# Summing the squares of the token norms on four column tiles and transposing the sums into columns, in a two-layer hybrid decoder trunk

## The chip, the cores and the metric

One core of one Trainium2 chip runs the whole program. The metric is the device time of one launch in microseconds (us), the median of several runs. A profiled execution is read beside them: it has its own time, a span from its first to its last instruction, and a trace of every instruction on the engines TensorE (PE; its weight loads are PEld), VectorE (DVE), ScalarE (ACT), GpSimd (POOL) and SyncE (SP, which issues the transfers).

## The reference, cut to what matters

The trunk has two layers over 512 tokens of width 1024. Each layer has a mixer (gated linear attention, mLSTM and Mamba-2 SSD, merged by gates) and a gated MLP with a causal convolution; both start from an RMSNorm of the residual stream.

```python
def rmsnorm(x, g):
    xf = x.astype(jnp.float32)
    y = xf * lax.rsqrt(jnp.mean(xf * xf, axis=-1, keepdims=True) + EPS)
    return (y * g).astype(x.dtype)

def reference(...):
    h = x
    for l in range(DEPTH):
        h = h + mixer_layer(rmsnorm(h, norm_mix[l]), w_in[l], ...)
        h = h + conv_ffn(rmsnorm(h, norm_ffn[l]), w_up[l], ...)
    return rmsnorm(h, norm_final)
```

The change touches the mean of squares and the inverse root of four of these five norms: the one ahead of the mixer and the one ahead of the MLP, in each of two layers. The final norm has its own code.

## The kernel before, in words

Activations lie with the channel on the partitions and the token along the free axis: 8 tiles of 128 x 512. Products are made in three passes of a split type: each float32 operand is cut into a high part and a remainder (`uh`/`ul` for activations, `wh`/`wl` for weights), and `wh x uh`, `wh x ul` and `wl x uh` are added in PSUM (`prods`). One unit of output, 128 channels by 512 tokens from 8 input tiles, is therefore 24 matmuls of 128 x 512.

The weights come from DRAM as raw tiles (`raw`, three buffers). Each is split on chip by `prep_`: ACT writes the high part (`wh`, line 354, seen in the trace as L230) and DVE the remainder (`wl`, line 355, seen as L233). A chunk is two units' weights; `wh` and `wl` have two buffers each (`W_BUFS = 2`), so the split of chunk c can start only when PE has read the last of chunk c - 2.

The norm's scale is not applied ahead of the products. The products use `h` times the gain, and each unit's result is multiplied by the inverse root (`rstd`, 128 x 512) when it leaves PSUM (`first`: the tiles `sm`, `cx`, `G` and others). While the tiles of `h` come, `square_tile` adds up their squares into one 128 x 512 tile `sq`. Then:

- `norm_end` (line 472) sums `sq` over its 128 partitions with `colsum` (line 790): for each of four blocks of 128 tokens one matmul with the block of `sq` as the weights and a column of ones as the moving operand, so that the sums land as four columns of 128 tokens (`m<-cst,sq`, 128 x 1). DVE scales them (`nx`, line 477) and makes the inverse root in ten short instructions (`rsqrt`, line 486: `rcol`, `nt`).
- `norm_rows_of_cols` (line 482) spreads the four columns `rcol` over all partitions with four transposes on PE (`m<-cst,rcol`, line 245), and ACT copies the result to `rstd`.

Both are called in `units` at a boundary, the first two units of a stage, as `mid`: `norm_end` in the middle of the pair, `norm_rows_of_cols` behind it. The instructions are placed on their engines by a scheduler, from the order of the program, the priorities that the code sets (`high_priority`) and the buffers, so a change in one place can move rows in others.

PSUM has two pools of four buffers, `pacc` (tiles `acc`) and `pm` (tiles `m`). Norm sums and transposes are always taken from `pm`. A unit's accumulator comes from `acc()`, and where `self.wide` is set (the first pair of a layer and the whole MLP) the pool depends on a running count of names:

```python
    def acc(self):
        self.n += 1
        if self.wide and self.n % 2:
            return self.mps()
        return self.pacc.tile([P, T], F32, tag="acc", name=f"acc_{self.n}")
```

`mps()`, `small()` and `t()` each add one to the same count. The column-tiled sum that the change uses is already in the kernel: `sums` (line 714) adds up squares for the heads' norms (`m<-sqo,cst`, 128 rows by 32 columns of weights, 128 moving columns). A float32 matmul shows as two records in the trace, a transpose as one.

Of the kernel before, what the change touches and what calls it, by code (L numbers as in the profile page):

```python
# [13 lines left out]
ALU = mybir.AluOpType  # L14
# [3 lines left out]
P = 128  # L18
L = 2
D = 1024  # L20
T = 512
KT = D // P
NB = T // P
EPS = 1e-6
# [109 lines left out]
class Kern:  # L134
# [337 lines left out]
    def norm_end(self):  # L472

        ps = self.mps()
        self.colsum(ps, 0, self.sq)
        x, rc, s = (self.small([P, NB], n) for n in ("nx", "rcol", "nt"))
        self.nc.vector.tensor_scalar(x, ps[:, 0:NB], 1.0 / D, EPS, op0=ALU.mult, op1=ALU.add)
        self.rsqrt(rc, x, s)
        self.rcol = rc
        self.sq = None  # L480
# [901 lines left out]
```

## Time and profile before

| | before |
|---|---|
| median of 3 runs | 2288.56 us (2288.24 to 2290.57) |
| profiled execution, its own time | 2289.48 us |
| its span | 2287.7 us |
| PE busy | 2274.1 us, 99% of the span, 10840 instructions |
| DVE busy | 1435.3 us, 63% |
| ACT busy | 904.6 us, 40% |
| mean granted TensorE clock | 0.999 |
| chain that ended last | 96% PE |

The busy share of PE says that it is nearly never without an instruction; since matmuls are pipelined, the distance from one start to the next (0.227 us for a 128 x 512 matmul here, while each shows as 0.39 us long) is what a matmul costs when nothing is waited for.

### The profile page before, as it was taken

To read this page: it belongs to the slowest core of one execution; us is meant where nothing else is said; L and a number is where in the kernel's file an instruction comes from. 1 tells how busy PE (TensorE), PEld (TensorE's weight loads), DVE (VectorE), ACT (ScalarE), POOL (GpSimd) and SP (SyncE) were. 2 spreads that over 40 slices of the span, in tenths; PEclk is the share of its full clock that TensorE was granted. 3 is DMA by queue.
4 is the path that set the end of the run, shared out by engine and by line. 5 is a ranking of instruction groups with operands and counts; after the bars stand their busy time and mean duration, and the time that the engine had idled before them with its cause. 6 is when DMAs were issued, how large, how long until landed. Compare 5 with 4: busy or idle time off the path is not lost.

```text
span 2287.7 us, 27324 instructions
## 1 busy us (share of the span) xinstructions
PE 2274.1 (99%) x10840; PEld 1874.6 (82%) x10840; DVE 1435.3 (63%) x2172; ACT 904.6 (40%) x1348; POOL 2.8 (0%) x22
## 2 busy tenths in 40 slices
PE   9999999999999999999999999999999999999998
PEld 7878888888888888888888788888888888888887
DVE  6977745474464587467579767355744745873774
ACT  6624532333333344234364345233333433442432
POOL 0000000000000000000000000000000000000000
PEclk9999999999999999999999999999999999999999
DMA  5253223232233433232323522222332343222222
GB/s 175 86 156 103 73 74 105 98 120 93 88 111 97 135 99 103 82 102 97 129 91 101 173 76 74 81 104 92 129 91 86 105 137 102 93 97 96 93 91 75
DMA packets 79136, 235.35 MB, mean 103 GB/s; under 512 B 9096, under 2 KB 12744, under 8 KB 79008
## 3 DMA queue, kind: packets, MB, share of 16 engines
q1 hardware_dynamic: 79008, 233.60, 31.5%
q8 instruction: 85, 1.39, 0.2%
q14 instruction: 43, 0.35, 0.0%
HBM read 229.16 MB, written 4.41 MB: 102 GB/s over the span
## 4 chain that ended last, share of the span: by engine, by line
PE 96%; DVE 2%; DMA 1%; ACT 1%; issue 0%; SPq 0%; DVEq 0%; ACTq 0%
PE acc L242 68%; PE m L242 27%; PE m L245 1%; DVE cc L239 1%; DVE wl L233 0%; DMA bc<-dr 0%; DMA h<-in_xT 0%; DMA eb<-dr 0%; ACT la L230 0%; DMA raw<-in_w 0%; DMA elb<-de 0%; DVE out L239 0%; DVE bc L861 0%; DVE sq L233 0%; ACT cc L230 0%
## 5 line engine op out<-in xcount | busy, mean ns | idle before, releaser
L230 ACT ACTIVATE wh<-raw 128x1024 fp32r<-128x1024 f32 (+2 forms) x372 | 384.9, 1077 | 567.9 <-PE acc L242 222.4
L242 PE MATMUL acc<-uh,wh 128*128 128x512 f32 x1536 | 601.3, 391 | 0.5 <-ACT wh L230 0.4
L242 PE MATMUL acc<-ul,wh 128*128 128x512 f32 x1536 | 600.2, 391 | 0.0
L242 PE MATMUL acc<-uh,wl 128*128 128x512 f32 x1536 | 599.2, 391 | 0.0
L233 DVE TENSOR_TENSOR wl<-raw,wh 128x1024 fp32r<-128x1024 f32 (+2 forms) x372 | 453.2, 1249 | 148.7 <-ACT wh L230 147.9
L242 PEld LDWEIGHTS acc<-uh,wh 128*128 128x128 f32 x1536 | 288.4, 188 | 60.5 <-ACT wh L230 1.0
L242 PEld LDWEIGHTS acc<-uh,wl 128*128 128x128 f32 x1536 | 288.4, 188 | 60.3 <-issue 1.0
L242 PEld LDWEIGHTS acc<-ul,wh 128*128 128x128 f32 x1536 | 288.4, 188 | 60.0 <-issue 1.1
L239 DVE SCALAR_TENSOR_TENSOR cc<-cx,par,cc 128x511 f32<-128x511 f32 (+2 forms) x296 | 217.4, 747 | 44.9 <-ACT cc L230 40.8
L242 PE MATMUL acc<-yl,wh 128*128 128x512 f32 x512 | 200.4, 391 | 0.0
L242 PE MATMUL acc<-yh,wh 128*128 128x512 f32 x512 | 199.5, 392 | 0.0
L242 PE MATMUL acc<-yh,wl 128*128 128x512 f32 x512 | 199.3, 390 | 0.0
L242 PE MATMUL m<-uh,wh 128*128 128x512 f32 x400 | 156.0, 391 | 1.3 <-ACT wh L230 1.3
L242 PE MATMUL m<-uh,wl 128*128 128x512 f32 x400 | 156.2, 391 | 0.1
L242 PE MATMUL m<-ul,wh 128*128 128x512 f32 x400 | 156.0, 390 | 0.1
L230 ACT ACTIVATE cc<-cx,par 128x512 f32<-128x512 f32 x128 | 102.7, 810 | 87.6 <-DVE cx L233 87.4
L242 PE MATMUL m<-ah,wl 128*128 128x512 f32 x308 | 120.0, 390 | 0.0
L242 PE MATMUL m<-al,wh 128*128 128x512 f32 x308 | 119.8, 389 | 0.0
L242 PE MATMUL m<-ah,wh 128*128 128x512 f32 x308 | 119.5, 389 | 0.0
L242 PEld LDWEIGHTS acc<-yh,wl 128*128 128x128 f32 x512 | 96.1, 188 | 20.3 <-issue 0.4
L242 PEld LDWEIGHTS acc<-yh,wh 128*128 128x128 f32 x512 | 96.1, 188 | 19.7
L242 PEld LDWEIGHTS acc<-yl,wh 128*128 128x128 f32 x512 | 96.2, 188 | 19.3
(213 smaller groups left out, 2662.2 us busy)
## 6 DMA issues: line engine op xcount, KB each, us to landing
raw<-in_w SPq DMA_DIRECT2D x336, 512.0 KB, 3.7
raw<-in_w SPq DMA_DIRECT2D x32, 704.0 KB, 4.1
bc<-dr SPq DMA_DIRECT2D x48, 256.0 KB, 3.8
h<-in_xT SPq DMA_DIRECT2D x16, 256.0 KB, 5.3
eb<-dr SPq DMA_DIRECT2D x32, 128.0 KB, 3.4
bc<-dn SPq DMA_DIRECT2D x16, 256.0 KB, 3.2
kept<-h SPq DMA_DIRECT2D x8, 256.0 KB, 2.0
h<-kept SPq DMA_DIRECT2D x8, 256.0 KB, 7.6
```

The lines of the kernel that those rows point to most:

```text
L230: return self.nc.scalar.activation(out, in_, func, bias=bias, scale=scale)
L233: return self.nc.vector.tensor_tensor(out, a, b, op=op)
L239: return self.nc.vector.scalar_tensor_tensor(out, a, s, b, op0=op0, op1=op1)
L242: return self.nc.tensor.matmul(out, lhsT, rhs, start=start, stop=stop)
L245: return self.nc.tensor.transpose(out, x, self.ident)
```

## The change

In `norm_end` the sums are taken by `sums` in place of `colsum`: four matmuls with 32 columns of ones as weights, each on its own 32 columns of the array, and a block of `sq` as the moving operand. Block b of 128 tokens then has its sums as 32 equal rows, partitions 32b to 32b + 31. DVE scales this 128 x 128 tile into a new SBUF tile `nrow`, PE transposes it, and DVE copies every 32nd column of the transpose into `nx`, which then holds what it held before. The inverse root and all that follows are the same. The new tile takes one more name from the count `self.n` in each of the four calls.

```diff
     def norm_end(self):
 
         ps = self.mps()
-        self.colsum(ps, 0, self.sq)
+        self.sums(ps, self.sq)
+        row = self.small([P, P], "nrow", 1)
+        self.nc.vector.tensor_scalar(row, ps[:, 0:P], 1.0 / D, EPS, op0=ALU.mult, op1=ALU.add)
+        self.transpose(ps[:, P:2 * P], row)
         x, rc, s = (self.small([P, NB], n) for n in ("nx", "rcol", "nt"))
-        self.nc.vector.tensor_scalar(x, ps[:, 0:NB], 1.0 / D, EPS, op0=ALU.mult, op1=ALU.add)
+        self.nc.vector.tensor_copy(x, ps[:, P:2 * P:32])
         self.rsqrt(rc, x, s)
```

The order of instructions moves in two kinds of places.

First, PE at the start of the MLP in layer 0 (layer 1 has the same pattern). Before: the boundary pair is `m_6044` and `m_6045` with the weights 6001/6002, the sums go to `m_6088`, the third unit is `acc_6149` with the second chunk's weights 6128/6129, and the transposes of the columns to `m_6114` come behind it.

```order
L242 MATMUL m_6088<-cst,sq_6037 128x1 x4
...
L242 MATMUL m_6045<-uh_893_6033,wh_6001 128x512
L242 MATMUL m_6045<-ul_893_6034,wh_6001 128x512
L242 MATMUL m_6045<-uh_893_6033,wl_6002 128x512
L242 MATMUL acc_6149<-uh_862_5780,wh_6128 128x512
L242 MATMUL acc_6149<-ul_862_5781,wh_6128 128x512
L242 MATMUL acc_6149<-uh_862_5780,wl_6129 128x512
...
L245 MATMUL m_6114<-cst,rcol_6094 128x128 x4
L242 MATMUL m_6188<-uh_862_5780,wh_6128 128x512
```

Now the same place on PE, with the boundary pair `acc_6047` and `m_6048` (weights 6004/6005), the second chunk's weights 6134/6135 and the third chunk's 6188/6189:

```order
L242 MATMUL m_6091<-sq_6040,cst 32x128 x4
...
L242 MATMUL m_6048<-uh_894_6036,wh_6004 128x512
L242 MATMUL m_6048<-ul_894_6037,wh_6004 128x512
L242 MATMUL m_6048<-uh_894_6036,wl_6005 128x512
L245 MATMUL m_6091<-cst,nrow_6096 128x128
L242 MATMUL acc_6234<-uh_863_5783,wh_6188 128x512
L242 MATMUL acc_6234<-ul_863_5784,wh_6188 128x512
L242 MATMUL acc_6234<-uh_863_5783,wl_6189 128x512
...
L245 MATMUL m_6120<-cst,rcol_6100 128x128 x4
L242 MATMUL m_6155<-uh_863_5783,wh_6134 128x512
```

The count is odd one step earlier, so the pools of the units are others: third and fourth unit are now both from `pm` (`m_6155`, `m_6194`), and they stand behind the transposes of the columns, whose tile `m_6120` is taken from the same pool ahead of them. The fifth unit, `acc_6234`, has moved ahead of them and follows the boundary pair directly, with the third chunk's weights.

On DVE at the same place, the remainders of that third chunk (`wl_6189`) stood behind the inverse root before and stand in it now:

```order
L477 TENSOR_SCALAR nrow_6096<-m_6091 128x128
L480 COPY nx_6099<-m_6091 128x4
L491 TENSOR_SCALAR rcol_6100<-nx_6099 128x4
L233 TENSOR_TENSOR nt_6101<-nx_6099,rcol_6100 128x4
L239 SCALAR_TENSOR_TENSOR nt_6101<-nt_6101,rcol_6100 128x4
L233 TENSOR_TENSOR wl_6189<-raw_6045,wh_6188 128x8x128
L239 SCALAR_TENSOR_TENSOR rcol_6100<-nt_6101,rcol_6100 128x4
L233 TENSOR_TENSOR wl_6189<-raw_6138,wh_6188 128x8x128
```

One row of the inverse root now stands between the two remainders, and six behind the second.

Second, ACT at the start of layer 0, before:

```order
L230 ACTIVATE wh_371<-raw_287 128x8x128
L230 ACTIVATE rstd_276<-m_277 128x512
L230 ACTIVATE wh_464<-raw_313 128x8x128
L230 ACTIVATE wh_464<-raw_375 128x8x128
L230 ACTIVATE zs_294<-sm_289,rbs_291,cst 128x512
```

and now (the tiles are the same ones, with numbers three or more higher):

```order
L230 ACTIVATE wh_374<-raw_290 128x8x128
L230 ACTIVATE wh_467<-raw_316 128x8x128
L230 ACTIVATE wh_467<-raw_378 128x8x128
L230 ACTIVATE rstd_279<-m_280 128x512
L230 ACTIVATE zs_297<-sm_292,rbs_294,cst 128x512
```

`rstd` moved behind a chunk's two splits, and on PE the transposes that feed it moved back by 14 matmuls; in layer 1 they moved back by 22. Later in both mixers the small matmuls of the SSD branch are grouped otherwise than before.

## Rows read from the trace of the kernel before

**Rows 1.** The page, busy time of each engine and the granted clock in 40 slices

```profile
PE 2274.1 (99%) x10840; PEld 1874.6 (82%) x10840; DVE 1435.3 (63%) x2172; ACT 904.6 (40%) x1348; POOL 2.8 (0%) x22
PEclk9999999999999999999999999999999999999999
```

**Rows 2.** Timeline, PE, MLP start of layer 0: start us, us, engine, line, operation

```profile
792.20 0.39 PE L242 MATMUL m<-ul,wh 128*128 128x512 f32 x1
792.43 0.95 PE L242 MATMUL m<-cst,sq 128*128 128x1 f32 x8
793.24 0.49 PE L242 MATMUL m<-uh,wl 128*128 128x512 f32 x1
...
793.80 0.40 PE L242 MATMUL m<-ul,wh 128*128 128x512 f32 x1
...
794.49 0.39 PE L242 MATMUL m<-ul,wh 128*128 128x512 f32 x1
794.72 0.40 PE L242 MATMUL m<-uh,wl 128*128 128x512 f32 x1
```

**Rows 3.** Timeline, PE, a column-tiled sum of the heads' norms, layer 0

```profile
312.43 0.39 PE L242 MATMUL acc<-ul,wh 128*128 128x512 f32 x1
312.75 0.43 PE L242 MATMUL m<-sqo,cst 128*32 128x128 f32 x8
...
313.67 0.39 PE L242 MATMUL acc<-ul,wh 128*128 128x512 f32 x1
```

**Rows 4.** Timeline, PE, two transposes between matmuls, layer 0

```profile
508.09 0.40 PE L242 MATMUL acc<-yh,wl 128*128 128x512 f32 x1
508.32 0.38 PE L245 MATMUL m<-cst,cc 128*128 128x128 f32 x2
...
509.01 0.39 PE L242 MATMUL acc<-yh,wl 128*128 128x512 f32 x1
```

**Rows 5.** Timeline, ACT and PE, start of layer 0

```profile
20.50 1.06 ACT L230 ACTIVATE wh<-raw 128x1024 fp32r<-128x1024 f32 x1 [1.63 <-DMA raw<-in_w]
20.60 0.95 PE L242 MATMUL m<-cst,sq 128*128 128x1 f32 x8
...
21.61 0.50 PE L242 MATMUL acc<-uh,wh 128*128 128x512 f32 x1
```

**Rows 6.** Timeline, DVE and ACT, MLP start of layers 0 and 1

```profile
793.41 0.16 DVE L477 TENSOR_SCALAR nx<-m 128x4 f32<-128x4 f32 x1 [5.54 <-PE m L242]
794.97 2.01 ACT L230 ACTIVATE wh<-raw 128x1024 fp32r<-128x1024 f32 x2 [8.67 <-issue]
796.06 2.36 DVE L233 TENSOR_TENSOR wl<-raw,wh 128x1024 fp32r<-128x1024 f32 x2 [0.51 <-ACT wh L230]
...
1924.60 0.16 DVE L477 TENSOR_SCALAR nx<-m 128x4 f32<-128x4 f32 x1 [5.54 <-PE m L242]
...
1927.25 2.36 DVE L233 TENSOR_TENSOR wl<-raw,wh 128x1024 fp32r<-128x1024 f32 x2 [0.51 <-ACT wh L230]
```

**Rows 7.** Timeline, ACT and PE, layer 0: a matmul that waited for a split

```profile
86.25 1.04 ACT L230 ACTIVATE wh<-raw 128x1024 fp32r<-128x1024 f32 x1
...
87.35 0.50 PE L242 MATMUL acc<-uh,wh 128*128 128x512 f32 x1 [0.43 <-ACT wh L230]
```

**Rows 8.** Timeline, layers 0 and 1: first evacuation, fifth accumulator's first matmul

```profile
41.83 0.68 DVE L233 TENSOR_TENSOR cx<-acc,rstd 128x512 f32<-128x512 f32 x1
...
45.27 0.39 PE L242 MATMUL acc<-uh,wh 128*128 128x512 f32 x1
...
1171.65 1.28 DVE L233 TENSOR_TENSOR cx<-acc,rstd 128x512 f32<-128x512 f32 x2
...
1179.66 0.39 PE L242 MATMUL acc<-uh,wh 128*128 128x512 f32 x1
```

**Rows 9.** Timeline, PE, SSD branch of layer 0: waits for DVE and ACT

```profile
170.80 0.40 PE L242 MATMUL m<-bc,xd 128*64 128x128 f32 x2 [1.06 <-DVE bc L233]
...
174.09 0.47 PE L242 MATMUL acc<-wh,uh 128*128 128x512 f32 x1 [0.39 <-ACT bc L230]
```

## The prediction

> **What bounds the kernel now.** The page comes first: PE is busy for 99% of the span and its granted clock stands at the upper level (2.4 GHz) throughout, while DVE has 63% and ACT 40% [rows 1]. So time can come from two places only: fewer or cheaper matmuls, or waits of PE that go or come. I then read the timeline of PE around the sums of squares. In a plain stretch one 128x512 matmul starts 0.227 us after the last (794.49 to 794.72 is one such step); the reader should see how much longer the step becomes around a small matmul [rows 2 to 4]. Last come the rows of ACT and DVE at the same places, since they split the weights that PE needs next [rows 5, 6]. The profiled execution took 2289.48 us, 0.92 above the median of the runs, 2288.56; the sum is made against 2289.48 and moved down by 0.92. A measurement of this kernel can tell about 0.2% from no change, which is 4.6 us.
>
> **The sums themselves.** Before, the matmul ahead of the sums starts at 792.20 and the third one behind them at 793.80: 1.60 us. Three plain steps are 0.68, so the column sums cost PE 0.92 [rows 2]. The column-tiled sum exists already, for the heads' norms: 312.43 to 313.67 is 1.24, less 0.68 is 0.56 [rows 3]. The new transpose has no row where it stands alone. Two transposes cost 508.09 to 509.01, 0.92, less 0.68, which is 0.24 [rows 4]; one lies between nothing and that, and since part of it is paid once for leaving and entering the products, I take 0.14. So a norm costs 0.70 on PE in place of 0.92, a gain of 0.22 (bounds 0.12 and 0.36). This is got at three of the four norms, 0.66 in all. At the first one PE waits anyway: its next product starts at 21.61, just as ACT ends the split begun at 20.50 [rows 5]. There the gain hides in that wait and the transpose adds its 0.14. Together: **-0.5 us**.
>
> Here a rule speaks against the change. The Trainium skill, page "TensorEngine Tiling (Array Packing)", section Instruction Overhead, says that each matmul has some 60 cycles of overhead and that one with a single column takes as long as one with 60, so that a dimension that is small already should not be given away. By an estimate from that page the eight one-column passes would need 8 x 25 ns, 0.20 us, a norm before would cost 0.31 on PE, and the term of the sums would be some +1.3 in place of -0.5. The rows decide otherwise: the eight passes hold PE from 792.43 to 793.24, 0.81 us, or 0.10 each [rows 2], and the eight of the tiled sum from 312.75 on are over sooner.
>
> **The new DVE work** is one 128x128 scaling and a 128x4 copy in place of a 128x4 scaling (0.16 [rows 6]), four times. It lies beside PE; what it does is make `rcol`, and so `rstd`, later. What that costs is taken up below.
>
> **The start of the MLP.** This is the large term. The order shows that in both layers the fifth unit (`acc_6234`) now follows the boundary pair directly, with the third chunk's weights. Those have the buffers of the first chunk (two buffers), so ACT may write them only when PE has read the first chunk's last high part. Before, that was harmless: the last such matmul started at 794.49, ACT began the split at 794.97, 0.48 later, DVE the remainders at 796.06 [rows 2, 6], and PE meanwhile had 48 matmuls of the second chunk to do. Now PE has none in between, since matmuls keep their order.
>
> I count from the start of that last high-part matmul. ACT starts at +0.48. A matmul that waited for such a split started 1.10 after the split did (86.25 to 87.35 [rows 7]), so the fifth unit starts at +1.58. It has two matmuls on high parts; the third needs the remainder. DVE starts that at +0.48 +1.09 = +1.57, needs half of 2.36, say 1.22 (two run slightly into each other) [rows 6], and with the same 0.06 of handover (86.25 +1.04 to 87.35) the third matmul starts at +2.85. Without a wait it would start at +1.05: 0.23 for the last product of the pair, 0.23 to the transpose, 0.14 for it, and two steps of 0.227. So PE loses **1.8 us**. Bounds: if remainders came at once, 1.58 - 0.60 = 1.0; if DVE did both remainders, or as much other work, ahead, 1.8 + 1.1 = 2.9. Layer 1 has the same order, and its rows before are spaced alike (`nx` to remainder 2.65 in both, 793.41 to 796.06 and 1924.60 to 1927.25 [rows 6]), so twice: **+3.6** (2.0 to 5.8). The inverse root is split by the two remainders and ends some 3 us later, but the transposes of its columns also come later, behind the delayed fifth unit's other 21 matmuls (4.8 us), so nothing waits for it.
>
> **The start of the mixers.** The transposes of `rcol` stand 14 matmuls later in layer 0 and 22 in layer 1: 3.2 and 5.0 us. `rstd` is later by that, and with it the evacuation of the accumulators. PE feels it only when it comes to the fifth accumulator, which needs the first one's buffer. In layer 0 that starts at 45.27 and the first evacuation ends at 41.83 + 0.68 = 42.51: 2.8 to spare. In layer 1 it is 1179.66 against 1172.3: 7.3 to spare [rows 8]. In layer 0 the two splits now ahead of `rstd` were behind it before, so DVE does the 2.4 us of remainders earlier and wins part of the 3.2 back; I put the evacuation about 2 later, inside the 2.8. Layer 1 loses 5 to 6 of 7.3. **Cost 0** (up to 2.9, below).
>
> **Sum:** -0.5 + 3.6 = +3.1; 2292.6 for the profiled kind, **2291.7** for the median. That is 0.14%, inside what can be told from no change.
>
> **The rivals.**
>
> *No wait at the MLP.* If the third chunk's split came sooner than I think, only the sums' gain is left: 2288.56 - 0.5 = 2288.1. For it: PE is busy for 99% and the scheduler chose this order. Against: ACT's start at 794.97 followed PE's last reading by one handover and not sooner [rows 2, 6], so the buffer is what it waited for. 0.13.
>
> *Late `rstd` in the mixer, slower than before.* Place: the fifth accumulator of layer 0. If DVE gains nothing from doing the remainders earlier, and they fall between `rcol` and `sm` in full, the evacuation is 3.3 + 2.4 = 5.7 later against 2.8 to spare: PE waits 2.9 more, and the total is +6.0, 2294.6. It decides from 1.5 us over the margin on, where the sum passes 4.6. For it: the order puts two splits ahead of `rstd`. Against: those rows were between `sm` and the first `cx` before. Layer 1 has 7.3 for 5.0 + 2.4. 0.15.
>
> *The column tiles do not overlap here*, so the change does not do what it says: the eight passes would cost as much as eight full ones, 0.10 each, 0.8 in place of 0.35 (312.75 to its next product), 0.45 more at each of four norms: 2291.7 + 1.8 = 2293.5. Against: the tiled sum in rows 3 runs in the same form. 0.02.
>
> *One-column sums are nearly free*, so replacing them costs. If the eight passes took no time of their own, a norm before would cost 0.92 - 0.81 = 0.11 and now 0.70: +0.59 at three norms and 0.14 at the first, +1.9 in place of -0.5, which gives 2294.1. Rows 2 speak against it, since PE starts nothing else in those 0.81. This is the mechanism that the page's rule above names. 0.01.
>
> *The SSD branch.* Its small matmuls are grouped otherwise in both layers. In layer 0 PE waits 1.06 and 0.39 there [rows 9]. These may go (2291.7 - 1.5 = 2290.2), or come in layer 1 too (2293.2). 0.07, half each.
>
> **How the numbers follow.** The forecast has 0.62; its own range, by ±0.6 on each of the two waits, is 2290.5 to 2293.0, with 0.06 of it above 2293.1, the bound of slower. Slower: 0.06 + 0.15 + 0.02 + 0.01 + 0.03 = 0.27. Faster than 2284.0 is reached by no case; 0.02 stays for what I don't see. The same: 0.71. The range takes in the case without waits at its low end, 2288.0, and the lower half of the late `rstd` at its high end, 2294.0.
>
> **What would show it.** In the changed profile the sums should stand as eight records of 128*32 for about 0.35 us to the next product, the `nrow` transpose alone for about 0.14. At both MLP starts the first matmul of the fifth unit should carry an idle of about 1 us released by ACT `wh`, and the third one of about 0.8 released by DVE `wl`. PE's list of waits should grow by some 3.6 us in these two lines. I am wrong if these waits are missing or far from 1.8 a layer, if PE waits at the fifth accumulator of a mixer, or if the total leaves the range by waits elsewhere.

## The result and the profile after

The kernel before took 2288.67 us (median of 4 runs, 2288.24 to 2290.57), the changed one 2301.84 (median of 4, 2301.20 to 2302.55): a ratio of 1.0054, 95% interval 1.0042 to 1.0066. It is 13.2 us slower, clear of what can be told from no change, and 8 us above the top of the predicted range. The profiled execution has a span of 2299.4 us, 11.7 more than before.

The page, busy time and granted clock, beside [rows 1]:

```profile
PE 2277.0 (99%) x10844; PEld 1873.0 (81%) x10844; DVE 1436.5 (62%) x2176; ACT 904.9 (39%) x1348; POOL 2.8 (0%) x22
PEclk9999999999999999999999999999999999999999
```

The work is the same: 4 more instructions on PE and 4 on DVE. So the time is in waits, and the list of PE's waits (engine, tile and line, what it waited for: us in total, times, longest) is where to look next:

```profile
PE acc L242 <- DVE gq L239: 5.4, 1, 5.4
PE acc L242 <- ACT wh L230: 2.7, 4, 0.9
PE acc L242 <- DVE wl L233: 1.6, 3, 0.5
...
PE acc L242 <- DVE cx L233: 0.3, 1, 0.3
```

All lines of it add up to 15.8 us, against 7.0 before. Of the second and third lines, 2.8 us are the predicted waits at the two MLP starts. The first line is a wait that was not foreseen.

**The MLP starts are as predicted.** Timeline of PE in the changed kernel, layer 0, where [rows 2] stood before:

```profile
798.01 0.39 PE L242 MATMUL m<-ul,wh 128*128 128x512 f32 x1
798.33 0.43 PE L242 MATMUL m<-sq,cst 128*32 128x128 f32 x8
798.68 0.50 PE L242 MATMUL m<-uh,wl 128*128 128x512 f32 x1
799.02 0.39 PE L242 MATMUL acc<-uh,wh 128*128 128x512 f32 x1
...
799.94 0.40 PE L242 MATMUL m<-ul,wh 128*128 128x512 f32 x1
800.17 0.39 PE L242 MATMUL m<-uh,wl 128*128 128x512 f32 x1
800.40 0.27 PE L245 MATMUL m<-cst,nrow 128*128 128x128 f32 x1
801.53 0.50 PE L242 MATMUL acc<-uh,wh 128*128 128x512 f32 x1 [0.86 <-ACT wh L230]
801.87 0.39 PE L242 MATMUL acc<-ul,wh 128*128 128x512 f32 x1
802.79 0.50 PE L242 MATMUL acc<-uh,wl 128*128 128x512 f32 x1 [0.53 <-DVE wl L233]
```

The sums: 798.01 to 799.02 is 1.01 for two steps of 0.227, so 0.56. The last matmul on the pair's high parts starts at 799.94, the fifth unit's third one at 802.79, 2.85 later; without a wait it would be 1.05 later. That is 1.8 us lost: 1.39 of it is idle time in the rows, the rest lies in the matmuls beside the waits, which take longer than a plain step. Layer 1 shows the same two waits at 1936.74 and 1938.00.

**The wait that was not foreseen** is in layer 0's mixer, 130 us behind the norm. There PE comes to the first accumulator of a token-major unit (`acc<-wh,uh`), which needs the buffer that the third `gq` still holds. DVE's timeline in the changed kernel:

```profile
171.54 0.68 DVE L864 TENSOR_SCALAR bc<-bc,ca 128x128 f32<-128x128 f32 x3 [0.83 <-DMA bc<-dr]
172.13 1.22 DVE L233 TENSOR_TENSOR wl<-raw,wh 128x1024 fp32r<-128x1024 f32 x1
173.27 1.06 DVE L864 TENSOR_SCALAR bc<-bc,ca 128x128 f32<-128x128 f32 x5
174.25 0.54 DVE L233 TENSOR_TENSOR eb<-eb,m 128x384 f32<-128x384 f32 x1
174.71 1.22 DVE L233 TENSOR_TENSOR wl<-raw,wh 128x1024 fp32r<-128x1024 f32 x1
175.85 0.68 DVE L239 SCALAR_TENSOR_TENSOR gq<-acc,rstd 128x512 f32<-128x512 f32 x1
```

and PE's, of which the first row answers to the last of [rows 9]:

```profile
176.67 0.76 PE L242 MATMUL acc<-wh,uh 128*128 128x512 f32 x1 [5.38 <-DVE gq L239]
177.23 0.63 PE L242 MATMUL acc<-wh,ul 128*128 128x512 f32 x1
177.66 0.63 PE L242 MATMUL acc<-wl,uh 128*128 128x512 f32 x1
...
179.37 0.54 PE L242 MATMUL acc<-wh,uh 128*128 128x512 f32 x1
179.74 0.39 PE L242 MATMUL acc<-wh,ul 128*128 128x512 f32 x1
```

Two things hold `gq` back. Two remainders of 1.22 us stand ahead of it on DVE, and so do scalings of rows (`bc`) that a transfer brings late. Before, both remainders stood behind `gq`:

```profile
172.48 0.87 DVE L861 TENSOR_SCALAR bc<-bc,ca 128x128 f32<-128x128 f32 x4
173.26 0.68 DVE L239 SCALAR_TENSOR_TENSOR gq<-acc,rstd 128x512 f32<-128x512 f32 x1
...
177.31 0.68 DVE L233 TENSOR_TENSOR gk<-acc,rstd 128x512 f32<-128x512 f32 x1
177.92 2.35 DVE L233 TENSOR_TENSOR wl<-raw,wh 128x1024 fp32r<-128x1024 f32 x2
```

The Trainium skill, page "PSUM — Partial Sum Buffer", section Engine vs sequencer instructions, says that the queues of ScalarE, VectorE and GpSimdE are strictly first in, first out; these rows agree, since PE had finished `gq`'s product by 171.3 us, and stood still, while `gq` waited its turn.

In the kernel before, `gq` had no time to spare there. The profile puts the 0.39 us that PE waited [rows 9] down to ACT's `bc`, but the matmul waits for both engines, and it started 0.15 behind the end of `gq` (173.94 to 174.09), as it does here (176.53 to 176.67) and in e6 below (174.55 to 174.69). So that wait reads as one for `gq` too, and what DVE does ahead of `gq` at this place is time that PE waits.

The rows come late because PE's small matmuls of the SSD branch stand later. The blocks as they were before, and as they are now, on PE and on the queue of SP that issues the transfers; before:

```profile
159.87 0.43 PE L242 MATMUL m<-bc,xd 128*64 128x128 f32 x2
...
161.99 1.57 SPq L516 DMA_DIRECT2D bc<-dr  x2
```

and in the changed kernel:

```profile
165.97 0.43 PE L242 MATMUL m<-bc,xd 128*64 128x128 f32 x2
...
168.09 0.91 SPq L519 DMA_DIRECT2D bc<-dr  x2
```

Between 160 and 172 us SP's waits for PE, ahead of `bc` transfers, are 4.4 us (one of 4.2) in the changed kernel and 0.2 before.

**The wait costs more than its length.** The windows of the stretch (us; busy us and instructions of each engine; granted clock, DMA share, GB/s):

```profile
176.67:179.37 2.70, 2.70 (x7) 2.12 (x7) 2.70 (x11) 0.63 (x1) 0.00 (x0) 0.50 0.79 284
179.74:184.00 4.26, 4.26 (x20) 3.19 (x18) 3.61 (x7) 0.53 (x2) 0.00 (x0) 1.00 0.18 62
```

Behind the wait the granted clock is 0.50, the lower of its two levels (1.2 GHz), and products start 0.43 apart. From 176.67 to 179.74 there are seven steps in 3.07 us, where 1.59 would do: 1.5 us more.

To account for the whole I took, in each profiled execution, the time from each product's start to the next product's, less 0.227 us (a product is a 128x512 matmul of split operands), and added it up over four stretches. It holds all waits, small matmuls and slow steps. (The table has the runs of the next section too; "layer 0" ends 204 us into the kernel before, "layer 1" is 1143 to 1327.)

| us beyond plain products | layer 0, first 700 products | MLP start 0 | layer 1, mixer start and SSD | MLP start 1 |
|---|---|---|---|---|
| before | 39.0 | 1.4 | 33.0 | 1.4 |
| after | 44.7 | 3.1 | 35.2 | 3.1 |
| e1 | 45.5 | 1.2 | 35.5 | 1.2 |
| e2 | 37.6 | 2.6 | 33.0 | 2.6 |
| e3 | 44.2 | 1.4 | 33.0 | 1.4 |
| e4 | 39.0 | 1.4 | 36.5 | 1.4 |
| e5 | 44.2 | 1.4 | 33.0 | 1.4 |
| e6 | 43.5 | 1.4 | 33.0 | 1.4 |
| e7 | 37.0 | 1.2 | 33.0 | 1.2 |
| e8 | 38.1 | 1.4 | 33.0 | 1.4 |
| e9 | 43.6 | 1.2 | 35.2 | 1.2 |

After less before: 5.7 + 1.7 + 2.2 + 1.7 = 11.3 of the 11.7 in span. Outside these stretches nothing differs by more than 0.2. Layer 0 varies by itself: before, e2, e4 and, but for two rows of PE, e7 have one and the same order there and show 37.0 to 39.0; the changed kernel, e1 and e3 share the new order and show 44.2 to 45.5.

### The profile page after: what moved, and what is told of

Same layout as the page of the kernel before. It is cut to its first block, busy times and chain, and to the rows that moved or that the text cites. A ratio compares the mean times of both kernels' runs of the same rounds, so it can differ in the third digit from the quotient of the medians.

```text
span 2299.4 us, 27339 instructions
## 1 busy us (share of the span) xinstructions
PE 2277.0 (99%) x10844; PEld 1873.0 (81%) x10844; DVE 1436.5 (62%) x2176; ACT 904.9 (39%) x1348; POOL 2.8 (0%) x22
## 3 DMA queue, kind: packets, MB, share of 16 engines
q8 instruction: 85, 1.39, 0.3%
## 4 chain that ended last, share of the span: by engine, by line
PE 92%; DVE 4%; ACT 2%; issue 1%; DMA 1%; SPq 0%; DVEq 0%; ACTq 0%
PE acc L242 64%; PE m L242 26%; DVE cc L239 1%; DVE wl L233 1%; PE m L245 1%; ACT la L230 0%; DMA raw<-in_w 0%; DMA bc<-dr 0%; ACT wh L230 0%; ACT zg L230 0%; DMA eb<-dr 0%; DVE cx L233 0%; ACT cc L230 0%; DVE xd L233 0%; DVE bc L864 0%
## 5 line engine op out<-in xcount | busy, mean ns | idle before, releaser
L239 DVE SCALAR_TENSOR_TENSOR cc<-cx,par,cc 128x510 f32<-128x510 f32 (+2 forms) x296 | 217.7, 747 | 44.8 <-ACT cc L230 40.8
```

Of the source, the lines that this page charges most:

```text
L239: return self.nc.vector.scalar_tensor_tensor(out, a, s, b, op0=op0, op1=op1)
```

## The experiments

Theory A: the sums are cheaper, and the scheduler's new order loses the time, in three places. Rival B: the running count alone does it. Rival C: the new chain makes each norm dearer on the chip, whatever the order.

**e1: the change, with the count as before.**

```diff
         row = self.small([P, P], "nrow", 1)
+        self.n -= 1
```

> The change as a whole, but the row of sums takes no number of its own, so that the pools of accumulators take turns as before; at the MLP starts the fifth unit then stands where it stood before. Theory A (the time went with PE's and DVE's new order: 3.5 us at the two MLP starts, 5 to 6 in the mixer of layer 0, 2 to 2.5 in that of layer 1): the 3.4 us of the MLP waits go, about 2298.3, and the 5.4 us wait of PE for gq stays. Rival B (the number is the cause of it all): 2288.7. Rival C (each of the four norms is dearer by 3.3 us through its own longer chain, whatever the order): 2301.8.

Measured: 2297.93 us against 2288.72, ratio 1.0040 [1.0025, 1.0055]. That is A's number. The MLP waits are gone (1.2 at both starts in the table), and the wait for `gq` stays:

```profile
PE acc L242 <- DVE gq L239: 5.1, 1, 5.1
```

So the parity of the count is 3.9 us of the 13.2, and B falls as the whole cause.

**e2: the kernel before, with only the count raised.**

```diff
         ps = self.mps()
         self.colsum(ps, 0, self.sq)
+        self.n += 1
```

> The kernel before with its column sums; only the running number is raised by one more in each norm. Nothing but the order at the two MLP starts moves. Theory A: two waits of 1.7 to 1.8 us each for the third chunk's split, 2288.7 + 3.5 = 2292.2. Rival B: all 13 us, 2301.8. Rival C: none, 2288.7.

Measured: 2291.44, ratio 1.0012 [1.0002, 1.0021]; +2.7. B is out. The waits are there with the old sums, but shorter: 1.2 a start in place of 1.7. PE's timeline in layer 0 shows why:

```profile
795.07 0.50 PE L242 MATMUL acc<-uh,wh 128*128 128x512 f32 x1 [0.96 <-ACT wh L230]
795.40 0.40 PE L242 MATMUL acc<-ul,wh 128*128 128x512 f32 x1
795.63 0.60 PE L245 MATMUL m<-cst,rcol 128*128 128x128 f32 x4
```

The inverse root is not delayed, so its transposes can follow here, and behind them stand the 48 matmuls of the third and fourth unit. The fifth unit's third matmul comes only at 806.98, when its remainder has long been made, and the second wait falls away.

**e3: the new sums in the first norm only, e4: in the third only**, the count as before in both. The other norms keep `colsum`.

```diff
+        self.norms = getattr(self, "norms", 0) + 1
+        new = self.norms in (1,)
+        if new:
...
+        else:
+            self.colsum(ps, 0, self.sq)
```

> The new sums and transpose in the first norm alone (layer 0's mixer), no number taken; the three others sum into columns as before. Theory A: the mixer of layer 0 alone has the new order, PE waits 5.4 us for gq behind two remainders, 5 to 6 us in all, about 2294.3. Rival B: 2288.7. Rival C: 2292.0.

Measured: 2296.09, ratio 1.0033 [1.0020, 1.0046]; +7.4, more than A's 5 to 6, with a wait of 5.3 for `gq`. B and C are both far off. This one norm makes more than half of the loss. (The table has 5.2 of the 7.4 in layer 0. Of the rest, 0.8 is that the profiled execution of the kernel before lies above its median, and 0.7 that PE's first product starts later in the one of e3.)

> The new sums and transpose in the third norm alone (layer 1's mixer), no number taken. Theory A: 2 to 2.5 us, about 2291.0, spread over the blocks of small matmuls of layer 1's SSD branch, without a wait of over 2 us. Rival B: 2288.7. Rival C: 2292.0.

Measured: 2291.78, ratio 1.0012 [1.0003, 1.0022]; +3.1. The total alone doesn't tell A from C. The trace does. All of it is in layer 1's stretch (36.5 against 33.0), where the norm is too; but up to 1200 us, with the sums, both transposes and the first evacuations, e4 is 0.2 us ahead of the kernel before, and up to 1300 us 0.8. The loss comes behind that, some 150 us after the norm. PE's waits there, 1140 to 1330 us, where there were none before:

```profile
PE m L242 <- DVE bc L233: 1.7, 2, 1.5
PE acc L242 <- ACT wh L230: 0.4, 1, 0.4
PE acc L242 <- ACT bc L230: 0.4, 1, 0.4
```

That is 2.5 of the 3.5; the rest is probably in blocks of small matmuls that are cut otherwise. In the changed kernel the same stretch has 1.0 of waits for a loss of 2.2. How the rest divides was not tried.

**e5: the old sums, the new order.** Three copies of four columns make the first norm's inverse root later; nothing else is changed.

```diff
+        if self.norms == 1:
+            self.nc.vector.tensor_copy(s, ps[:, 0:NB])
+            for _ in range(2):
+                self.nc.vector.tensor_copy(x, s)
+                s, x = x, s
+            self.nc.vector.tensor_scalar(x, s, 1.0 / D, EPS, op0=ALU.mult, op1=ALU.add)
```

> The kernel before, column sums in all four norms; in the first one three copies of 128x4 stand between the sums and the inverse root, so that it comes later, and that gives layer 0 the order that the new sums gave it (the first norm's neighbourhood and some SSD rows near the end of the branch apart). Theory A (the order is what costs): PE waits about 5.3 us for the third gq and the total is that of the new sums in the first norm alone, 2296.1, within 1. Rival C (tiled sums and transpose themselves cost): at most 0.5 above the kernel before, 2289.2.

Measured: 2294.70, ratio 1.0026 [1.0016, 1.0036]; +6.2. It is 1.4 below e3, a little outside the 1 that I allowed, and 5.5 above C's number. The mechanism is there in full without a tiled sum or a new transpose in the kernel:

```profile
PE acc L242 <- DVE gq L239: 5.2, 1, 5.2
```

**e8: the same with one copy.** The loop of two copies is left out.

> As the run with three copies, but only one copy of 128x4 stands between the first norm's column sums and its inverse root: the inverse root is still later than before, by one small operation, while nearly all of layer 0's order stays that of the kernel before (the third gq stands ahead of the token chunk's remainders). Theory A: no wait for gq, 2288.5 within 0.7. If it is the later inverse root as such that costs, and not the order, a third of the 6.2 of three copies: 2290.6.

Measured: 2288.65 against 2288.61, ratio 0.9998 [0.9988, 1.0007]. PE never waits for `gq`. A little later costs nothing; two copies more, and the scheduler puts the remainders ahead of `gq`, for 6 us. The loss goes with the order and not in proportion to the delay.

**e6: e3 with the remainders behind `gq`.** The split of that one chunk is held until the third `gq` is issued.

```diff
+        if c < len(self.chunks) and self.chunks[c][:3] == (2, TOK[1], 1):
+            with self.tc.issue_after(self.gq2.ins), self.tc.high_priority(PREP_PRIO):
+                self.prep_()
+            return
```

> The new sums in the first norm alone, as in the earlier run of 2296.1, but the split of the second half of the second token chunk of layer 0 is held until the third gq is issued: on DVE its two remainders (1.22 us each) stand behind gq instead of ahead of it. Theory A: PE's wait for gq falls from 5.3 by 2.3 to about 3.0, so 2293.8, and up to 1.5 less if the granted clock then stays at its upper level behind the wait (2292.3). Rival D (the late row transfers of the SSD branch are all of it, and the remainders only fill DVE's idle time): the wait stays at 5, 2296.1.

Measured: 2293.46, ratio 1.0020 [1.0011, 1.0030]; 2.6 less than e3, inside A's range, and D is out as the whole cause. But the wait fell by 1.6 to 3.64, not by 2.3. DVE's timeline:

```profile
170.98 0.87 DVE L878 TENSOR_SCALAR bc<-bc,ca 128x128 f32<-128x128 f32 x4 [0.52 <-DMA bc<-dr]
172.60 0.87 DVE L878 TENSOR_SCALAR bc<-bc,ca 128x128 f32<-128x128 f32 x4 [0.75 <-DMA bc<-dr]
173.39 0.55 DVE L233 TENSOR_TENSOR eb<-eb,m 128x384 f32<-128x384 f32 x1
173.86 0.69 DVE L239 SCALAR_TENSOR_TENSOR gq<-acc,rstd 128x512 f32<-128x512 f32 x1
174.46 2.35 DVE L233 TENSOR_TENSOR wl<-raw,wh 128x1024 fp32r<-128x1024 f32 x2
```

With the first remainder gone, DVE waits for the second row transfer instead (0.75), which the remainder had covered. So D holds for what is left: the late rows. Moving them by themselves was not tried, and that part rests on the trace alone. The granted clock still fell behind a wait of 3.64: products from 175.34 to 177.90 start 0.43 apart. The 2.6 of the medians is not seen in full in the profiled executions, which differ by 1.3 (2295.76 and 2294.45): at `gq`, wait and slow steps together give back 1.8, and 0.6 of it is lost again behind that place.

**e7: the new sums ahead of the MLPs only**, with `self.norms in (2, 4)` and the count as before.

> The new sums and transpose in the two norms ahead of the MLPs only, no number taken, so that no order in the mixers moves and the fifth unit stays where it was. Theory A: 0.2 us won at each, 2288.7 - 0.4 = 2288.3, not to be told from no change by the total, but to be read in PE's steps at the two MLP starts (0.56 for the sums and 0.14 for the transpose in place of 0.92, and no wait). Rival C (each norm is dearer by 3.3): 2295.3.

Measured: 2287.92, ratio 0.9997 [0.9988, 1.0006], 0.6 below the kernel before and not to be told from it. The steps tell it. PE's timeline, layer 0:

```profile
790.62 0.39 PE L242 MATMUL m<-ul,wh 128*128 128x512 f32 x1
790.94 0.43 PE L242 MATMUL m<-sq,cst 128*32 128x128 f32 x8
791.30 0.50 PE L242 MATMUL m<-uh,wl 128*128 128x512 f32 x1
791.63 0.39 PE L242 MATMUL m<-uh,wh 128*128 128x512 f32 x1
...
795.97 0.39 PE L242 MATMUL acc<-ul,wh 128*128 128x512 f32 x1
796.20 0.27 PE L245 MATMUL m<-cst,nrow 128*128 128x128 f32 x1
796.23 0.47 PE L242 MATMUL acc<-uh,wl 128*128 128x512 f32 x1
796.54 0.39 PE L242 MATMUL acc<-uh,wh 128*128 128x512 f32 x1
```

1.01 less two steps is 0.56 for the sums; 795.97 to 796.54 is 0.57, less two steps 0.12 for the transpose. 0.68 in place of 0.92 [rows 2], without a wait. C falls.

**e9: the whole change with both repairs**, that of e1 and that of e6.

> The whole change with two repairs: the row of sums takes no number, and the split of the second half of the second token chunk of layer 0 is held until the third gq is issued. Theory A (the parts add up): the whole change without its number, 2297.9, less the 2.6 that holding the split won with the first norm alone: 2295.3. If the parts act on one another, anything from 2293 to 2297.9. Left over by theory A: late row transfers in layer 0, some 4, and layer 1's mixer, some 3.

Measured: 2296.19, ratio 1.0031 [1.0020, 1.0043]. A's 2295.3 lies inside the interval, and so does 2297.9, the time with nothing won; the hold won 1.7 here against 2.6 in e6. That it did win is seen in the wait for `gq`, which fell from 5.1 to 3.1.

The parts add up: e2's 2.7, e3's 7.4 and e4's 3.1, less e7's 0.6, make 12.6 of the 13.2. No version here beats the kernel before by more than a measurement can tell. The one that keeps the gain and none of the loss is e7.

## Why the prediction was wrong, point by point

- **The sums: right.** 0.56 and 0.12 where 0.56 and 0.14 were forecast, against 0.92; e1 and e7 show 0.2 less at each MLP start. The rule of the Trainium skill, page "TensorEngine Tiling (Array Packing)", section Instruction Overhead, that a matmul with one column takes as long as one with 60, would by the estimate in the prediction have made the new sums the dearer ones; e7's steps speak against it, as [rows 2] did.
- **The MLP waits: right in place, mechanism and size.** The third matmul comes 2.85 behind the last high-part matmul, as worked out; 3.6 was forecast for both layers, and removing the two waits in e1 gave back 3.9 (3.8 in the table). That nothing waits for the late `rstd` there holds too.
- **The rivals of the hardware** (tiles that don't overlap, one-column sums nearly free) are out by e7; the case without a wait at the MLP is out by the trace.
- **The start of the mixers: the step that failed.** "PE feels it only when it comes to the fifth accumulator" holds for that accumulator: the first evacuation came 2.25 us later, at 44.08 to 44.76, where about 2 was forecast, and PE started there without a wait at 45.26. The rival of a slower `rstd`, at 0.15, is out by that. (The 0.3 us for `cx` in the list of waits comes at 56.60, two accumulators further on.) It does not hold for the rest. With the later `rstd` came another order from there on, and e5 shows that a later inverse root alone is enough for it; how the scheduler got there was not followed. 130 us further down it put two remainders ahead of an evacuation and PE's SSD blocks 6 us later. The cost of 0 was some 6 to 7 in layer 0 (e3, e5) and 2 to 3 in layer 1 (e4 and the changed kernel), which is about the 10 us between the forecast of +3.1 and the 13.2 measured. For layer 1 there is no run like e5, so that the order is the cause there rests on where the trace of e4 has the loss.
- **The SSD branch, rival at 0.07: right place, wrong size.** It was priced at 1.5 us by the two waits that the profile of before shows [rows 9]. Those were no bound. The second of them stands at the very matmul that waits 5.4 us in the changed kernel; read as a wait for ACT, as the profile has it, it does not show that `gq` had nothing to spare. Nor were they steady: in e2 and e4, whose order there is the one of before, the first of them, 1.06, is 0.5 and 0.8, and in e7 and e8, where the order is nearly so, it is absent. The grouping had been noticed, and DVE's order there was not followed to the accumulator that `gq` frees.

## What to carry to other kernels

When a change makes an early value later in a scheduled kernel, compare the order of every engine to the end of the stage, not only around the edit, and at each accumulator that PE needs again ask what stands ahead of its evacuation on the evacuating engine, and whether the evacuation had time to spare in the old profile. Price such a place by the work queued ahead of the evacuation plus the slow steps behind the wait, not by the waits of the old profile. A change in a running count or a few small operations put into the old kernel (e2, e5, e8) tells cheaply whether the order or the new arithmetic costs.

## What was not expected of the hardware

A wait of 5.4 us cost PE 1.5 more behind it, because the granted clock came back at 0.50: seven steps of about 0.43 in place of 0.227. In e5, behind 5.2, eleven steps from 175.84 on did the same, so the price of such a wait is not fixed. It happened behind 3.6 in e6 and behind 3.1 in e9, and in e9 the clock fell only when PE was at work again: it was 1.00 from 174.49 to 175.72, for five products, and 0.50 from 176.06 to 179.04. The first wait of [rows 9], 1.06, shows no such steps. The waits of 0.9 at the MLP starts left the clock alone too: the products behind 803.13 start 0.23 to 0.24 apart.
